# Weight buffers and activations in opposite 64-byte halves of SBUF

## The chip, the core and the metric

The kernel runs on one core of a Trainium2 chip. What is measured is the device time of one execution in microseconds (us). The kernel before takes 2329.44 us, the median of three runs (2329.22 to 2330.43).

## What is computed

The kernel computes a decoder trunk of two layers on 256 tokens of width 2048, in float32. Cut to the frame:

```python
h = x                                            # (1, 256, 2048)
for layer in range(2):
    u = rms_norm(h, norm_mix) @ w_in             # 2048 x 6160 (layer 0), 2048 x 7176 (layer 1)
    a, b = two_mixers(u)                         # layer 0: GLA and MoBA; layer 1: FoX and HGRN2
    h = h + concat([a, b]) @ w_out               # 2048 x 2048
    m = rms_norm(h, norm_mlp)
    h = h + square(relu(m @ w_up)) @ w_down      # 2048 x 8192, 8192 x 2048
return rms_norm(h, final_norm)
```

Two details matter for the change. MoBA adds an ALiBi bias, `-slope * (t - s)` under a causal mask, to its scores. FoX adds differences of a running sum of log forget gates over the 256 positions, `cumsum(log_f)`.

## The kernel before

**Three products for one.** Every large product is made of float32r matmuls. A weight tile `raw` is split into `wh` (rounded to float32r, ScalarE, L996) and `wl = raw - wh` (VectorE, L997), an activation in the same way into a high and a low part, and each product is high x wh + high x wl + low x wh, summed in PSUM.

**Units and blocks.** A unit is 128 rows of a weight matrix times 1024 columns (1040 or 1032 in the two blocks that carry a few extra columns, `extra`). A block is 16 units that sum into one set of accumulators; there are 49 blocks, 784 units. `fetch` (L981 to L998) loads the units in pairs into a `raw` buffer (three of them) and splits each into a `wh` and a `wl` buffer (six of each, handed out in turn). `fetch` runs two units ahead.

**Where the matmuls stand.** The loop at the end calls, for unit i, `step(0, i)` and then `step(1, i - 2)`: the first half of unit i's output (token rows or hidden columns), then the second half of unit i - 2. So between the first matmul of `step(0, i)` and that of `step(0, i + 1)` stand the matmuls of two units of one parity. There are two kinds:

- natural blocks (L1040): the activation is stationary (128 x 128) and the weights move, 512 columns at a time; 6 matmuls a step. In the blocks of `w_in` the activation is `xh` and `xl`; in those of `w_out` and `w_down` it is `mh0`, `ml0` for units 0 to 7 of a block and `mh1`, `ml1` for units 8 to 15.
- turned blocks (L1023, the sixteen of `w_up`): the weights are stationary and `xh` or `xl` moves, 256 columns at a time; 12 matmuls a step.

**Where the tiles lie.** The pools lay tiles one after another in each partition, every one at a multiple of 32 bytes. In the program as built these are the addresses, in bytes modulo 128:

| tiles | before | after |
|---|---|---|
| `wh` and `wl`, buffers 0, 2, 4 | 0 | 64 |
| `wh` and `wl`, buffers 1, 3, 5 | 64 | 64 |
| from one such buffer to the next | 4160 bytes | 4224 bytes |
| `raw` (three buffers) | 0 | 64 |
| `xh`, `xl`, `h`, `ident` | 0 | 0 |
| `mh0`, `ml0`, `ml1` | 0 | 0 |
| `mh1` | 64 | 0 |
| `stg` (two buffers) | 64 | 0 |
| `lev`, `at` | 0 | 64 |
| `v`, `sv`, `g` (tags S1, S2) | 0 | 64 |

Units 0, 2, 4, ... of a block use buffers 0, 2, 4 and units 1, 3, 5, ... buffers 1, 3, 5, since 16 is even. Inside a weight tile the matmuls start at multiples of 512 bytes, inside `xh`, `xl`, `mh`, `ml` too.

**Beside the matmuls** run the mixers' tasks, which the loop hands out in small pieces between units (`bg`). Three of them are touched: the constants made at the start (`const_task`), the ALiBi bias (`alibi`, L783, on GpSimd), and the running sum of the forget gates (`fox_forget`, three small matmuls with the triangular matrix `tri`, L803 to L805).

Of the kernel before, what the change touches and what calls it, by code (L numbers as in the profile page):

```python
# [8 lines left out]
F32 = mybir.dt.float32  # L9
F32R = mybir.dt.float32r  # L10
# [7 lines left out]
D = 2048  # L18
KT = D // P
CB = 1024  # L20
LAG = 2
AHEAD = 2
STARTN = 14
# [14 lines left out]
def trunk(ctx: ExitStack, tc: tile.TileContext, x, ev_norm_mix, ev_w_in, ev_gla_gate_w2, ev_gla_gate_b,  # L38
# [66 lines left out]
    def small(shape, name, bufs=2):  # L105
        return work.tile(shape, F32, name=name, tag=name, bufs=bufs)
# [11 lines left out]
    xl = cons.tile([P, KT, S], F32R, name="xl")  # L118
    h = cons.tile([P, 2, D], F32, name="h")
    mtiles.update({m: cons.tile([P, 256], U8, name=f"mask{m}") for m in LEVELS[4:]})  # L120
    tri = cons.tile([P, S], F32, name="tri")
    seg = cons.tile([P, S], F32, name="seg")

    dist = cons.tile([P, 384], F32, name="dist")


    xin = x[0].rearrange("(t p) d -> p t d", p=P)
# [41 lines left out]
    pool.memset(mhalf, -0.5)  # L169
    masks = {}  # L170

    def causal(tl):
        for c in (0, 256):
            pool.affine_select(out=tl[:, c:c + P], in_=tl[:, c:c + P], pattern=[[-1, P]], compare_op=ALU.is_ge,
                               fill=NEG, base=0, channel_multiplier=1)

    def const_task():

        pool.memset(tri, 1.0)
        pool.affine_select(out=tri[:, 0:P], in_=tri[:, 0:P], pattern=[[1, P]], compare_op=ALU.is_ge, fill=0.0, base=0,  # L180
                           channel_multiplier=-1)
        pool.memset(seg, 1.0)
        pool.memset(seg.rearrange("p (a b) -> p a b", b=64)[:, :, 0:1], 0.0)
        for m in LEVELS[1:]:
            yield from room(0, 1)
            nb = 64 // m
            mf = lev()[:, 0:64]
            mk = mtiles[m]
            mv = mf.rearrange("p (n m) -> p n m", m=m) if 1 < m < 64 else mf
            dims = [[2 * m, nb]] * (nb > 1) + [[0, m]] * (m > 1)  # L190
            pool.memset(mf, 1.0)
            pool.affine_select(out=mv, in_=mv, pattern=[[-a, b] for a, b in dims], compare_op=ALU.is_ge, fill=0.0,
                               base=0, channel_multiplier=1)
            pool.affine_select(out=mv, in_=mv, pattern=dims, compare_op=ALU.is_ge, fill=0.0, base=m - 1,
                               channel_multiplier=-1)
            yield BAR
            dve.tensor_copy(mk.rearrange("p (g c) -> p g c", c=64), mf.unsqueeze(1).to_broadcast([P, 4, 64]))
            lev_done()
            masks[m] = mk
            yield 0.3  # L200
        pool.iota(dist[:, 0:128], pattern=[[1, 128]], base=0, channel_multiplier=-1,
                  allow_small_or_imprecise_dtypes=True)
        pool.iota(dist[:, 128:384], pattern=[[1, 256]], base=-128, channel_multiplier=-1,
                  allow_small_or_imprecise_dtypes=True)
        causal(dist)
        yield BAR
        mx, e0, e1, sm = (small([P, 8], f"lb{i}", 1) for i in range(4))
        dve.tensor_tensor(mx, vec("lb0"), vec("lb1"), ALU.max)
        dve.tensor_sub(e0, vec("lb0"), mx)
        dve.tensor_sub(e1, vec("lb1"), mx)  # L210
        act.activation(e0, e0, AF.Exp)
        act.activation(e1, e1, AF.Exp)
        dve.tensor_add(sm, e0, e1)
        dve.reciprocal(sm, sm)
        dve.tensor_mul(e0, e0, sm)
        dve.tensor_mul(e1, e1, sm)
        dve.tensor_add(lb, e0, e1)
        dve.tensor_sub(lb, lb, e0)
        yield 1.0
# [26 lines left out]

    def norm_rstd(key):
        until(lambda: all((key, "ss", t, i) in written for t in range(2) for i in range(2)))
        r = small([P, 2], "rstd")
        pool.tensor_add(r, ssq[key][:, :, 0], ssq[key][:, :, 1])  # L250
        rsq(r, r, 2, 1.0 / D)
        return r
# [198 lines left out]
    def gla_out(at, v, g, dv, h0, nh, k0, gain, halves, key):  # L451

        yield from room(1)
        ps = aux()
        for i in range(nh):
            hd = h0 + i
            dg, off = at[hd // 2 * 2]
            c = slice(hd * dv, (hd + 1) * dv)
            o0 = ps[:, i * 2 * dv:i * 2 * dv + dv]
            o1 = ps[:, i * 2 * dv + dv:(i + 1) * 2 * dv]  # L460
            pe.matmul(o0, dg[:, 2 * (hd % 2)], v[:, 0, c], start=True, stop=True)
            pe.matmul(o1, off[:, hd % 2], v[:, 0, c], start=True, stop=False)
            pe.matmul(o1, dg[:, 2 * (hd % 2) + 1], v[:, 1, c], start=False, stop=True)
        yield BAR
        yield from room(0, 1)
        n = 2 * nh
        ss = small([P, 4], "oss")
        y = lev()
        for j in range(n):
            act.activation(y[:, j * dv:(j + 1) * dv], ps[:, j * dv:(j + 1) * dv], AF.Square, accum_out=ss[:, j:j + 1])  # L470
        yield BAR
        r = small([P, 4], "orr")
        rsq(r[:, 0:n], ss[:, 0:n], n, 1.0 / dv)
        yield BAR
        y = y.rearrange("p (t c) -> p t c", t=2)
        for j in range(n):
            i, t = divmod(j, 2)
            c = slice((h0 + i) * dv, (h0 + i + 1) * dv)
            dve.scalar_tensor_tensor(y[:, t, i * dv:(i + 1) * dv], ps[:, j * dv:(j + 1) * dv], r[:, j:j + 1],
                                     g[:, t, c], ALU.mult, ALU.mult)  # L480
        aux_done()
        yield 0.8
        yield BAR
        yield from room(1)
        pt = aux()
        for i in range(2):
            for t in range(2):
                pe.transpose(pt[:, i * 256 + t * P:i * 256 + (t + 1) * P], y[:, t, i * P:(i + 1) * P], ident)
        lev_done()
        yield BAR  # L490
        if 0 not in halves:
            halves[0] = mid(0)
        mh, ml = halves[0]
        for i in range(2):
            gg = gain[:, i:i + 1] if gain.shape[1] == 2 else gain[:, 0:1]
            act.activation(mh[:, k0 + i], pt[:, i * 256:(i + 1) * 256], AF.Identity, scale=gg)
        for i in range(2):
            gg = gain[:, i:i + 1] if gain.shape[1] == 2 else gain[:, 0:1]
            dve.scalar_tensor_tensor(ml[:, k0 + i], pt[:, i * 256:(i + 1) * 256], gg,
                                     mh[:, k0 + i].bitcast(F32), ALU.mult, ALU.subtract)  # L500
            written.add((key, k0 + i))
        aux_done()
        yield 0.8
# [78 lines left out]
    def mixers(lay):  # L582
# [33 lines left out]
        def gla_qk(acc, t):  # L616
            if t == 0:
                scales()
                st["q"] = scratch("mh0", 4, "gqT")
                kb = scratch("ml0", 8, "gkT")  # L620
                st["k"], st["b"] = kb[:, 0:4], kb[:, 4:8]
                st["d"] = small([P, 8, 2], "gdiag", 1)[:, 0:4]
            sg = stage()
            act.activation(sg[:, 0:512], acc[0], AF.Identity, scale=st["rq"][:, t:t + 1])
            dve.tensor_scalar(sg[:, 512:1024], acc[1], st["r"][:, t:t + 1], None, ALU.mult)
            tk["q", t] = spawn(heads_gen(sg, 0, 4, st["q"], t))
            tk["k", t] = spawn(heads_gen(sg, 4, 4, st["k"], t))

            def diag():
                yield from room(0, 1)  # L630
                junk = lev()
                for hd in range(4):
                    a, b = (sg[:, c + hd * P:c + (hd + 1) * P] for c in (0, 512))
                    dve.tensor_tensor_reduce(out=junk[:, hd * P:(hd + 1) * P], in0=a, in1=b, scale=1.0, scalar=0.0,
                                             op0=ALU.mult, op1=ALU.add, accum_out=st["d"][:, hd, t:t + 1])
                    yield 0.2
                lev_done()
            tk["d", t] = spawn(diag())
# [142 lines left out]
                                            tk["out"]))  # L781

        def alibi(hd, bt):  # L783
            pool.tensor_scalar(bt, dist, 2.0 ** -(hd + 1), None, ALU.mult)
            yield 0.05

        def fox_forget():
# [12 lines left out]
            yield BAR  # L800
            yield from room(1)
            pc = aux()
            pe.matmul(pc[:, 0:8], tri[:, 0:P], l[:, 0], start=True, stop=True)  # L803
            pe.matmul(pc[:, 8:16], tri[:, P:S], l[:, 0], start=True, stop=False)
            pe.matmul(pc[:, 8:16], tri[:, 0:P], l[:, 1], start=False, stop=True)  # L805
            yield BAR
            ct = small([P, 2, 8], "fct", 1)
            act.copy(ct, pc[:, 0:16].rearrange("p (t h) -> p t h", h=8))
# [172 lines left out]
    def fetch(i):  # L981
# [9 lines left out]
        raw = raws["cur"][:, j % 2]  # L991
        if i < 2:
            nc.sync.dma_start(raw, w[r0:r0 + P, cs])
        wh = wspl.tile([P, n], F32R, name="wh", tag="wh")
        wl = wspl.tile([P, n], F32R, name="wl", tag="wl")
        pin(act.activation(wh, raw, AF.Copy))  # L996
        pin(dve.tensor_sub(wl, raw, wh.bitcast(F32)))  # L997
        split[i] = (wh, wl)  # L998
# [117 lines left out]
```

## Time and profile before

| what | value |
|---|---|
| median of three runs | 2329.44 us |
| profiled execution, its own time | 2329.49 us |
| its span in the trace | 2327.8 us |
| TensorE busy | 2308.9 us, 99% |
| VectorE busy | 1285.5 us, 55% |
| ScalarE busy | 1086.3 us, 47% |
| GpSimd busy | 63.3 us, 3% |
| weights and activations moved | 418.68 MB, mean 180 GB/s |
| granted TensorE clock, mean | 0.998 |

A matmul's busy time in the trace overlaps that of the next, so the share says that TensorE always has work, not how fast it goes through it. In the timeline each row merges neighbouring instructions of one kind; its first number is the start of the first of them.

### The profile page before, as it was taken

The page shows a single profiled execution, that of the slowest core. Times are in us where ns is not written, and L with a number is a line of the kernel's source. Part 1 is how long each engine was busy: PE and PEld are TensorE (multiplying, and loading weights), DVE is VectorE, ACT ScalarE, POOL GpSimd, SP SyncE. Part 2 cuts the span into 40 slices and gives each one's busy share as a digit, 9 for nine tenths or more (in the row PEclk, how much of TensorE's full clock was granted, in tenths as well). Part 3 has the DMA queues.
Part 4 walks back from the last instruction along what each step waited for, and adds up shares of the span by engine and source line. Part 5 has one row for each costly group of instructions (what it writes and reads, how often), then busy time and mean ns, then how long its engine had stood idle before and what let it go on. Part 6 is the DMA issues. An engine that isn't in the chain of part 4 may idle for free.

```text
span 2327.8 us, 32679 instructions
## 1 busy us (share of the span) xinstructions
PE 2308.9 (99%) x13652; PEld 2026.2 (87%) x13652; DVE 1285.5 (55%) x1564; ACT 1086.3 (47%) x1370; POOL 63.3 (3%) x128
## 2 busy tenths in 40 slices
PE   8999999999999999999999999999999999999998
PEld 7888888998998998998887888788988988988986
DVE  5575545554554454465557775555554554555554
ACT  5464544443443353354446545644443443443443
POOL 2000100000000000000000000100000000000000
PEclk9999999999999999999999999999999999999999
DMA  7645545555555555555554434455555565555553
GB/s 242 193 150 162 163 159 185 181 183 198 182 192 188 189 191 186 194 183 184 183 180 160 162 127 163 150 183 187 186 186 195 183 194 185 192 188 191 189 184 124
DMA packets 110612, 418.68 MB, mean 180 GB/s; under 512 B 6814, under 2 KB 8944, under 8 KB 110336
## 3 DMA queue, kind: packets, MB, share of 16 engines
q1 hardware_dynamic: 109536, 415.46, 54.0%
q8 instruction: 107, 1.75, 0.3%
q10 hardware_dynamic: 608, 1.06, 0.1%
q14 instruction: 41, 0.34, 0.0%
q0 software_dynamic: 320, 0.07, 0.0%
HBM read 414.47 MB, written 2.10 MB: 179 GB/s over the span
## 4 chain that ended last, share of the span: by engine, by line
PE 98%; ACT 1%; DVE 1%; DMA 0%; SPq 0%; issue 0%; POOL 0%; POOLq 0%; ACTq 0%
PE acc L1040 61%; PE acc L1023 31%; PE aux L434 1%; PE aux L1040 1%; PE aux L273 1%; PE aux L335 0%; DMA raw<-in_ev_w_in_dram 0%; PE aux L512 0%; PE aux L536 0%; DVE hb L737 0%; ACT wh L996 0%; PE aux L511 0%; PE aux L427 0%; PE aux L558 0%; PE aux L557 0%; PE aux L367 0%
## 5 line engine op out<-in xcount | busy, mean ns | idle before, releaser
L997 DVE TENSOR_TENSOR wl<-raw,wh 128x1024 fp32r<-128x1024 f32 (+2 forms) x784 | 960.2, 1226 | 891.9 <-ACT wh L996 890.3
L996 ACT ACTIVATE wh<-raw 128x1024 fp32r<-128x1024 f32 (+2 forms) x784 | 830.3, 1060 | 1130.6 <-PE acc L1040 675.6
L1040 PE MATMUL acc<-wh,mh 128*128 128x512 f32 x1280 | 414.0, 394 | 0.0
L1040 PE MATMUL acc<-wh,ml 128*128 128x512 f32 x1280 | 412.4, 393 | 0.0
L1040 PE MATMUL acc<-wl,mh 128*128 128x512 f32 x1280 | 412.1, 393 | 0.0
L1023 PE MATMUL acc<-xh,wl 128*128 128x256 f32 x2048 | 353.9, 280 | 0.0
L1023 PE MATMUL acc<-xh,wh 128*128 128x256 f32 x2048 | 353.5, 279 | 0.0
L1023 PE MATMUL acc<-xl,wh 128*128 128x256 f32 x2048 | 353.1, 279 | 0.0
L1023 PEld LDWEIGHTS acc<-xh,wh 128*128 128x128 f32 x2048 | 290.6, 188 | 2.6
L1023 PEld LDWEIGHTS acc<-xh,wl 128*128 128x128 f32 x2048 | 289.5, 188 | 0.7
L1023 PEld LDWEIGHTS acc<-xl,wh 128*128 128x128 f32 x2048 | 289.0, 189 | 0.0
L1040 PEld LDWEIGHTS acc<-wh,ml 128*128 128x128 f32 x1280 | 240.2, 188 | 55.0
L1040 PEld LDWEIGHTS acc<-wl,mh 128*128 128x128 f32 x1280 | 240.4, 188 | 54.2
L1040 PEld LDWEIGHTS acc<-wh,mh 128*128 128x128 f32 x1280 | 238.0, 188 | 53.9 <-DVE stg L892 1.6
L1040 PE MATMUL acc<-wh,xh 128*128 128x512 f32 x832 | 272.3, 398 | 2.4 <-ACT xh L279 2.4
L1040 PE MATMUL acc<-wl,xh 128*128 128x512 f32 x832 | 262.9, 387 | 2.5 <-DVE wl L997 2.5
L1040 PE MATMUL acc<-wh,xl 128*128 128x512 f32 x832 | 261.7, 385 | 0.0
L1040 PEld LDWEIGHTS acc<-wl,xh 128*128 128x128 f32 x832 | 153.2, 189 | 34.2 <-DVE wl L997 3.8
L1040 PEld LDWEIGHTS acc<-wh,xl 128*128 128x128 f32 x832 | 153.2, 189 | 31.1
L1040 PEld LDWEIGHTS acc<-wh,xh 128*128 128x128 f32 x832 | 147.8, 189 | 28.6 <-ACT xh L279 3.3
L867 DVE TENSOR_TENSOR h<-acc,h 128x512 f32<-128x512 f32 x72 | 47.8, 685 | 20.5 <-PE acc L1040 20.5
L892 DVE SCALAR_TENSOR_TENSOR stg<-acc,rrow 128x512 f32<-128x512 f32 x64 | 42.4, 685 | 17.2 <-PE acc L1023 17.2
(239 smaller groups left out, 1006.1 us busy)
## 6 DMA issues: line engine op xcount, KB each, us to landing
raw<-in_ev_w_up_dram SPq DMA_DIRECT2D x64, 1024.0 KB, 4.9
raw<-in_ev_w_down_dram SPq DMA_DIRECT2D x64, 1024.0 KB, 5.5
raw<-in_od_w_up_dram SPq DMA_DIRECT2D x64, 1024.0 KB, 4.9
raw<-in_od_w_down_dram SPq DMA_DIRECT2D x64, 1024.0 KB, 5.5
raw<-in_od_w_in_dram SPq DMA_DIRECT2D x48, 1024.0 KB, 4.9
raw<-in_ev_w_in_dram SPq DMA_DIRECT2D x39, 1024.0 KB, 5.4
raw<-in_ev_w_out_dram SPq DMA_DIRECT2D x16, 1024.0 KB, 5.6
raw<-in_od_w_out_dram SPq DMA_DIRECT2D x16, 1024.0 KB, 5.5
```

What stands on the lines that cost most here:

```text
L273: pin(pe.transpose(ps[:, i * 256 + t * P:i * 256 + (t + 1) * P], h[:, t, kt * P:(kt + 1) * P], ident))
L434: pe.matmul(ps[:, i * 64:(i + 1) * 64], a, r, start=True, stop=True)
L867: dve.tensor_tensor(h[:, t, sl], acc[i], h[:, t, sl], ALU.add)
L892: dve.scalar_tensor_tensor(y, acc[i].rearrange("p (k s) -> p k s", s=S), 0.0, rr, ALU.max, ALU.mult)
L996: pin(act.activation(wh, raw, AF.Copy))
L997: pin(dve.tensor_sub(wl, raw, wh.bitcast(F32)))
L1023: pe.matmul(banks[o][:, k * S:(k + 1) * S], m[:, c0:c0 + P], a, start=j == 0 and p == 0 and k == 0, stop=j == n - 1 and p == 2 and k == 1, ...
L1040: pin(pe.matmul(o, a, m[:, c0:c1], start=first, stop=last))
```

## The change

All large weight buffers are made 4224 bytes long (`WB = 1056` columns of 4 bytes), of which 1024 to 1040 columns are used. The tiles ahead of them are cut so that the first buffer starts at 64 modulo 128; small tiles behind them grow so that the activations start at 0. `tri` keeps one 128 x 128 triangle instead of a triangle and a block of ones, and the ones are read with step 0 from a tile `one`. `dist` keeps 256 of its 384 columns; `alibi` multiplies these and copies the first 128 into the last 128.

```diff
+WB = 1056
...
-    tri = cons.tile([P, S], F32, name="tri")
+    tri = cons.tile([P, P], F32, name="tri")
+    one = cons.tile([P, 8], F32, name="one")
     seg = cons.tile([P, S], F32, name="seg")
 
-    dist = cons.tile([P, 384], F32, name="dist")
+    dist = cons.tile([P, 256], F32, name="dist")
+    cons.tile([P, 8], F32, name="pad2")
...
+        pool.memset(one, 1.0)
         pool.memset(tri, 1.0)
-        pool.affine_select(out=tri[:, 0:P], in_=tri[:, 0:P], pattern=[[1, P]], compare_op=ALU.is_ge, fill=0.0, base=0,
+        pool.affine_select(out=tri, in_=tri, pattern=[[1, P]], compare_op=ALU.is_ge, fill=0.0, base=0,
                            channel_multiplier=-1)
...
-        pool.iota(dist[:, 128:384], pattern=[[1, 256]], base=-128, channel_multiplier=-1,
+        pool.iota(dist[:, 128:256], pattern=[[1, 128]], base=-128, channel_multiplier=-1,
                   allow_small_or_imprecise_dtypes=True)
-        causal(dist)
+        causal(dist, (0,))
...
-        r = small([P, 2], "rstd")
+        r = small([P, 16], "rstd")[:, 0:2]
...
-        ss = small([P, 4], "oss")
+        ss = small([P, 16], "oss")
...
-                st["d"] = small([P, 8, 2], "gdiag", 1)[:, 0:4]
+                st["d"] = small([P, 16, 2], "gdiag", 1)[:, 0:4]
...
-            pool.tensor_scalar(bt, dist, 2.0 ** -(hd + 1), None, ALU.mult)
+            pool.tensor_scalar(bt[:, 0:256], dist, 2.0 ** -(hd + 1), None, ALU.mult)
+            pool.tensor_copy(bt[:, 256:384], bt[:, 0:128])
...
-            pe.matmul(pc[:, 0:8], tri[:, 0:P], l[:, 0], start=True, stop=True)
-            pe.matmul(pc[:, 8:16], tri[:, P:S], l[:, 0], start=True, stop=False)
-            pe.matmul(pc[:, 8:16], tri[:, 0:P], l[:, 1], start=False, stop=True)
+            pe.matmul(pc[:, 0:8], tri, l[:, 0], start=True, stop=True)
+            pe.matmul(pc[:, 8:16], one[:, 0:1].to_broadcast([P, P]), l[:, 0], start=True, stop=False)
+            pe.matmul(pc[:, 8:16], tri, l[:, 1], start=False, stop=True)
...
-        wh = wspl.tile([P, n], F32R, name="wh", tag="wh")
-        wl = wspl.tile([P, n], F32R, name="wl", tag="wl")
+        wh = wspl.tile([P, WB], F32R, name="wh", tag="wh")[:, 0:n]
+        wl = wspl.tile([P, WB], F32R, name="wl", tag="wl")[:, 0:n]
```

On VectorE, ScalarE and the DMA queue of SyncE the instructions stand in the same order before and after. On GpSimd the only rows that move are those of the constants and of the ALiBi biases. Before, the eight biases of layer 0 (`lev<-dist`) stand there in this way, between the output norms of the last GLA heads (`orr`) and the norm of the next stage (`rstd`):

```order
L245 TENSOR_TENSOR orr<-orr,mhalf 128x2
L784 TENSOR_SCALAR lev<-dist 128x384 x3
L244 TENSOR_SCALAR orr<-oss 128x2
L245 TENSOR_TENSOR orr<-orr,mhalf 128x2
L784 TENSOR_SCALAR lev<-dist 128x384 x5
L250 TENSOR_TENSOR rstd<-ssq 128x2
```

After, at the same place on GpSimd:

```order
L788 TENSOR_SCALAR lev<-dist 128x256 x2
L789 COPY lev<-lev 128x128 x2
L788 TENSOR_SCALAR lev<-dist 128x256
L248 TENSOR_SCALAR orr<-oss 128x2
L789 COPY lev<-lev 128x128
L249 TENSOR_TENSOR orr<-orr,mhalf 128x2
L788 TENSOR_SCALAR lev<-dist 128x256
L789 COPY lev<-lev 128x128
L788 TENSOR_SCALAR lev<-dist 128x256
L789 COPY lev<-lev 128x128
L788 TENSOR_SCALAR lev<-dist 128x256 x2
L789 COPY lev<-lev 128x128 x2
```

Each bias has become a shorter multiply and a copy; one multiply stands ahead of a norm that it followed with its copy behind. On TensorE one row differs in what it reads, the second of the three small matmuls of the forget gates in layer 1 (`fxl` is the log gate). After, it stands among its neighbours so:

```order
L1045 MATMUL acc_10009<-wh,xl 128x512
L1045 MATMUL acc_10010<-wh,xl 128x512
L808 MATMUL aux<-fxl,tri 128x8
L809 MATMUL aux<-fxl,one 128x8
L810 MATMUL aux<-fxl,tri 128x8
L339 MATMUL aux<-ident,stg 128x128 x4
```

Before, the same rows read `tri` three times, at the same place; nothing on TensorE has moved.

## Rows read from the trace of the kernel before

**Rows 1.** Page, part 1: busy us (share of the span) x instructions, by engine.

```profile
PE 2308.9 (99%) x13652; PEld 2026.2 (87%) x13652; DVE 1285.5 (55%) x1564; ACT 1086.3 (47%) x1370; POOL 63.3 (3%) x128
```

**Rows 2.** Largest waits of TensorE: for what, us in total, times, longest.

```profile
PE aux L1052 <- DMA vrow<-in_ev_norm_mix_dram: 3.7, 1, 3.7
PE acc L1040 <- DVE wl L997: 2.5, 2, 2.2
```

**Rows 3.** Timeline of VectorE around 1250 us: start us, us, instruction.

```profile
1246.42 4.54 DVE L737 TENSOR_TENSOR_SCAN hb<-seg,hb 128x256 f32<-128x256 f32 x5
1250.88 1.35 DVE L997 TENSOR_TENSOR wl<-raw,wh 128x1024 fp32r<-128x1024 f32 x1
```

**Rows 4.** Page, part 5: groups, count | busy, mean ns | idle before.

```profile
L1040 PE MATMUL acc<-wh,mh 128*128 128x512 f32 x1280 | 414.0, 394 | 0.0
...
L1023 PE MATMUL acc<-xh,wh 128*128 128x256 f32 x2048 | 353.5, 279 | 0.0
...
L1040 PE MATMUL acc<-wh,xh 128*128 128x512 f32 x832 | 272.3, 398 | 2.4 <-ACT xh L279 2.4
```

**Rows 5.** Timeline of TensorE, second up block of layer 0.

```profile
458.27 0.36 PE L1023 MATMUL acc<-xh,wh 128*128 128x256 f32 x1
...
477.95 0.62 PE L1023 MATMUL acc<-xh,wh 128*128 128x256 f32 x4
...
480.67 0.62 PE L1023 MATMUL acc<-xh,wh 128*128 128x256 f32 x4
...
483.51 0.64 PE L1023 MATMUL acc<-xh,wh 128*128 128x256 f32 x4
...
486.29 0.64 PE L1023 MATMUL acc<-xh,wh 128*128 128x256 f32 x4
...
489.13 0.63 PE L1023 MATMUL acc<-xh,wh 128*128 128x256 f32 x4
```

**Rows 6.** Timeline of TensorE, first down block of the third hidden quarter, layer 0.

```profile
870.89 0.62 PE L1040 MATMUL acc<-wh,mh 128*128 128x512 f32 x2
...
873.66 0.62 PE L1040 MATMUL acc<-wh,mh 128*128 128x512 f32 x2
...
876.41 0.64 PE L1040 MATMUL acc<-wh,mh 128*128 128x512 f32 x2
...
879.21 0.62 PE L1040 MATMUL acc<-wh,mh 128*128 128x512 f32 x2
...
881.97 0.63 PE L1040 MATMUL acc<-wh,mh 128*128 128x512 f32 x2
...
893.08 0.63 PE L1040 MATMUL acc<-wh,mh 128*128 128x512 f32 x2
...
895.84 0.62 PE L1040 MATMUL acc<-wh,mh 128*128 128x512 f32 x2
...
898.62 0.63 PE L1040 MATMUL acc<-wh,mh 128*128 128x512 f32 x2
...
901.39 0.39 PE L1040 MATMUL acc<-wh,mh 128*128 128x512 f32 x1
```

**Rows 7.** Groups by shape, the splits on VectorE; page, part 5, on ScalarE.

```profile
L997 DVE TENSOR_TENSOR wl<-raw,wh 128x1024 fp32r<-128x1024 f32 x752 | 920.7, 1225 | 853.2 <-ACT wh L996 851.6
...
L997 DVE TENSOR_TENSOR wl<-raw,wh 128x1040 fp32r<-128x1040 f32 x16 | 19.8, 1242 | 18.3 <-ACT wh L996 18.3
...
L996 ACT ACTIVATE wh<-raw 128x1024 fp32r<-128x1024 f32 (+2 forms) x784 | 830.3, 1060 | 1130.6 <-PE acc L1040 675.6
```

**Rows 8.** DMA issues: count, KB each, median us to landing.

```profile
raw<-in_ev_w_in_dram SPq DMA_DIRECT2D x39, 1024.0 KB, 5.4
...
raw<-in_ev_w_in_dram SPq DMA_DIRECT2D x8, 1040.0 KB, 5.4
```

**Rows 9.** Groups on GpSimd.

```profile
L784 POOL TENSOR_SCALAR lev<-dist 128x384 f32<-128x384 f32 x8 | 10.3, 1306 | 40.0 <-PE aux L536 33.5 <-PE aux L488 6.4
...
L394 POOL COPY lev<-hb 128x128 f32<-128x128 f32 x4 | 1.5, 386 | 18.3 <-PE aux L434 18.3
```

More of the change, by code (lines that the diff above doesn't have):

```diff
@@ L170, in trunk, with causal @@
     masks = {}
-    def causal(tl):
-        for c in (0, 256):
+    def causal(tl, cs=(0, 256)):
+        for c in cs:
             pool.affine_select(out=tl[:, c:c + P], in_=tl[:, c:c + P], pattern=[[-1, P]], compare_op=ALU.is_ge,
```

## The prediction

> **What bounds the kernel now.** I read the page's busy table first: TensorE is busy 99% of the span, VectorE 55%, ScalarE 47% [rows 1]. Then TensorE's waits, of which the two largest are 3.7 us for a first load at the start and 2.5 us for wl [rows 2]; 2.2 of these fall at 1250 us, where VectorE is first held by a row of scans [rows 3]. So the time is the number of matmuls times the distance from one start to the next, and the costliest groups give the numbers [rows 4]: 3 x 2048 = 6144 turned matmuls of 256 columns (weights stationary, xh or xl moving), 3 x 1280 = 3840 of 512 columns on mh or ml, 3 x 832 = 2496 of 512 columns on xh or xl (weights moving, activations stationary). The mean durations there overlap their neighbours; the pace has to be read from start times. So the view that matters is TensorE's timeline.
>
> The kernel before already holds both layouts side by side. A weight buffer is 4160 bytes, that is 65 x 64, so buffers 0, 2, 4 start at 0 mod 128 bytes and 1, 3, 5 at 64. Six buffers are handed out in turn and a block has 16 units, so even units of a block lie at 0 and odd units at 64. xh and xl lie at 0. mh0, ml0 and ml1 lie at 0, mh1 alone at 64.
>
> In an up block [rows 5] each row is the first of a unit's stretch of 24 matmuls; counted from the block's first matmul at 458.27 us, 477.95 begins unit 7. The differences are 2.72 (odd), 2.84 (even), 2.78 (odd), 2.84 us (even). Even: 5.68 us / 48 = 118.3 ns a matmul; odd: 5.50 / 48 = 114.6 ns. With weights in the other 64-byte half than xh and xl, a matmul is 3.75 ns faster.
>
> That could be a habit of odd units rather than of addresses. The down block [rows 6] tells these apart; a unit is 12 matmuls there and 870.89 begins unit 4. Units 4 to 7 read mh0 and ml0, both at 0: 2.77 and 2.80 us for even units (232.1 ns a matmul), 2.75 and 2.76 for odd ones (229.6 ns). Units 12 to 14 read mh1 at 64 and ml1 at 0: 2.76 and 2.77 for even units (230.4 ns), 2.78 for the odd one (231.7 ns). The order has turned round, and what turned is mh1's half. Four of six matmuls there are on mh1, so even units gain in most of them and odd ones lose. I take the relation between the two operands of TensorE as the cause: same half slow, other half fast.
>
> The Trainium skill's "SBUF — State Buffer", section "Who interferes with whom", states that TensorE has two read ports, for the moving operand and for the weight load, independent of each other, and that only the pair shared by VectorE and GpSimd causes contention. By that the halves could not matter and the change would give nothing; rows 5 and 6 disagree by 2.5 to 3.75 ns a matmul, and I go by the rows.
>
> **The change part by part.** After it all wh and wl buffers lie at 64 and xh, xl, mh0, ml0, mh1, ml1 at 0 mod 128, so every large matmul has the relation of the fast units.
>
> Turned matmuls: half of 6144 are in even units, 3072 x 3.75 ns = 11.5 us. Bounds from single pairs of rows 5: 2.84 against 2.78 is 2.5 ns (7.7 us), 2.84 against 2.72 is 5.0 ns (15.4 us).
>
> Matmuls on mh and ml: the four kinds of units are equally many and average (232.1 + 229.6 + 230.4 + 231.7) / 4 = 230.95 ns; all become the 229.6 of the odd early unit. 3840 x 1.35 ns = 5.2 us. Bounds: if the end value is 2.76 us a unit (230.0 ns), 3.6 us; if 2.75 (229.2 ns), 6.7 us.
>
> Matmuls on xh and xl with the weights moving: no long clean stretch of these is in my rows, since transposes and score matmuls of the mixers stand between. Their addresses are those of units 4 to 7 of rows 6, so half of 2496 go from 232.1 to 229.6: 1248 x 2.5 ns = 3.1 us; bounds by single pairs, 0.01 us and 0.05 us a unit, 1.0 to 5.2 us.
>
> VectorE and ScalarE read raw, which moves from 0 to 64. An odd unit's row of a 1040-column pair already began at 4160 bytes, 64 mod 128. Such pairs take 1242 ns a unit on VectorE against 1225 with 1024 columns, which is 17 ns for 16 columns more; ScalarE takes 1060 ns a unit over all [rows 7]. I cost the move at nothing: a unit is at least 2.72 us of TensorE, so on either engine even a tenth more stays hidden. The loads of these pairs landed in 5.4 us, the same as the plain ones of that matrix [rows 8]: nothing.
>
> GpSimd: each alibi bias was one multiply of 384 columns, 1.31 us, eight times; it becomes one of 256 and a copy of 128 columns, for which a copy of that size in layer 1 took 0.39 us [rows 9]. With the shorter multiply anywhere between nothing and 1.31 us, that is 0.9 us less to 0.4 us more a head, so at most 8 x 0.4 = 3 us on GpSimd; none of it is TensorE's, which has other matmuls then and has nothing of GpSimd's among its large waits [rows 2]. The ones and the smaller sum matrix and distance table cost nothing: GpSimd, 3% busy [rows 1], makes the constants early, and one 8-column matmul reads ones instead of a half of tri.
>
> Transposes: stg moves from 64 to 0 and lev from 0 to 64, against the identity at 0. In the program 112 lose and 80 gain; at the turned price of 3.75 ns that is 0.4 us against 0.3. Nothing.
>
> What may be late next is the wait of 2.2 us for wl, behind the scans of layer 1's gates on VectorE [rows 2, 3]. A block of 192 matmuls before it becomes about 0.2 us shorter, so the wait may grow by that. Elsewhere splits stay two units ahead.
>
> Sum: 11.5 + 5.2 + 3.1 = 19.8 us off the profiled execution's own 2329.5 us (span 2327.8 and 1.7 around it; the median of the runs is 2329.4): 2309.7, so I say 2310. All low ends together give 12.3 us (2317), all high ends 27.3 us (2302).
>
> **The rivals.** First, no change: the pace alternates with the unit for a reason that stays, say the row of the raw pair or the turn of the buffers, and the padding does nothing. For it: in up blocks parity and half can't be separated. Against it: the reversal in rows 6. It gives 2329. 5%. The independent ports of the Trainium skill's "SBUF — State Buffer" (the section above) would give the same.
>
> Second, slower: what has to lie apart is the weights and raw. Raw was at 0 throughout, so weights at 64 (odd units) were apart from it; after the change raw is at 64 too, and every unit would have the even units' pace. Turned: 3072 x 3.75 = 11.5 us more; mh and ml: from 230.95 to 232.1, 4.4 us more; the rest 3.1 more: 2348. It decides if ScalarE's and VectorE's reads of raw, which run beside nearly every matmul, disturb TensorE. For it: again parity in the up blocks. Against: in units 12 and 14 raw and the weights are both at 0, and those units are the fast ones. 4%.
>
> Third, less than the sum: the pace of a fast unit is partly owed to its slow neighbours (TensorE's queue of loaded weights evens out distances), or the gain holds for turned matmuls alone. That gives 2329.5 - 11.5 = 2318 or a little above, up to 2325. 6%.
>
> **How the numbers follow.** The forecast, with the bounds above, gets 85%, of which I leave 3% for below 2302. The range is 2302 to 2318: the ends of the sum, with 1 us above for the wait of layer 1. What a measurement here can tell from no change is 0.2%, 4.7 us. Faster by more: forecast and third rival, 0.91. Within: 0.05. Slower: 0.04.
>
> **What would show it.** In the profile after: stretches of 24 turned matmuls at about 2.75 us in every unit, with no alternation, and of 12 matmuls in down blocks at about 2.755 us throughout both halves of a block; an up block of 384 about 0.7 us shorter, a down block of 192 about 0.26 us. TensorE's waits stay those of before, and splits keep 1.06 and 1.23 us. It is wrong if units still alternate (first rival), if all take 2.84 us (second), or if the stretches are shorter but a new wait stands in TensorE's list.

## The result and the profile after

The kernel after takes 2313.97 us (median of 6 runs, 2313.8 to 2314.34), the kernel before 2329.33 us beside it (6 runs, 2328.4 to 2330.43): a ratio of 0.9935 [0.9924, 0.9945], 15.4 us less. The forecast was 2310 with a range of 2302 to 2318. The time falls into the range, but the profile shows that the 15.4 us are not the sum that was forecast: one term is larger, two are missing. All runs of this document that were profiled had a granted clock of 0.998 or 0.999 of the full one.

Page of the kernel after, part 1, answering to [rows 1]; its span is 2312.3 us, 15.5 less:

```profile
PE 2293.0 (99%) x13652; PEld 2009.5 (87%) x13652; DVE 1285.3 (56%) x1564; ACT 1086.5 (47%) x1370; POOL 62.2 (3%) x136
```

TensorE's largest waits in it (what for, us in total, times, longest), answering to [rows 2]:

```profile
PE aux L1057 <- DMA vrow<-in_ev_norm_mix_dram: 3.7, 1, 3.7
PE acc L1045 <- ACT xh L283: 3.1, 2, 2.4
PE acc L1045 <- DVE wl L1002: 2.6, 3, 2.2
```

TensorE is still busy 99%, and no wait has come in: 3.7 us for the first load, 2.6 (before 2.5) for `wl` with the longest at 2.2 as before, 3.1 for `xh` at the starts of stages (before 2.4). So the whole gain is in the distance from one matmul's start to the next.

Timeline of TensorE in the second up block of layer 0 (start us, busy us, instruction), answering to [rows 5]. The first row is the block's first matmul, the next five are the first of the stretches of units 7 to 11, the last is the first matmul of the next block:

```profile
457.80 0.34 PE L1028 MATMUL acc<-xh,wh 128*128 128x256 f32 x1
...
477.22 0.62 PE L1028 MATMUL acc<-xh,wh 128*128 128x256 f32 x4
...
479.94 0.62 PE L1028 MATMUL acc<-xh,wh 128*128 128x256 f32 x4
...
482.66 0.62 PE L1028 MATMUL acc<-xh,wh 128*128 128x256 f32 x4
...
485.38 0.62 PE L1028 MATMUL acc<-xh,wh 128*128 128x256 f32 x4
...
488.10 0.62 PE L1028 MATMUL acc<-xh,wh 128*128 128x256 f32 x4
...
501.71 0.39 PE L1045 MATMUL acc<-wh,mh 128*128 128x512 f32 x1
```

Every stretch of 24 takes 2.72 us: 113.3 ns a matmul, with no alternation between even and odd units. Before, even units took 118.3 and odd units 114.6. The block takes 501.71 - 457.80 = 43.91 us; before, from 458.27 to 503.05, 44.78. That the once fast odd units are faster too was not forecast.

In the first up block of a hidden quarter (here the second quarter of layer 0) it begins otherwise; the rows are the first of units 3 to 6:

```profile
598.87 0.63 PE L1028 MATMUL acc<-xh,wh 128*128 128x256 f32 x4
...
601.70 0.63 PE L1028 MATMUL acc<-xh,wh 128*128 128x256 f32 x4
...
604.52 0.62 PE L1028 MATMUL acc<-xh,wh 128*128 128x256 f32 x4
...
607.24 0.62 PE L1028 MATMUL acc<-xh,wh 128*128 128x256 f32 x4
```

Units 3 and 4 take 2.83 and 2.82 us (117.7 ns), one of either parity, and from unit 5 on a stretch takes 2.72. Six of the eight hidden quarters begin in this way. In the first quarter of each layer it is the second up block that runs at 118.0 and 117.7 ns in units 1 and 2 and at 113.3 to 113.4 from unit 3 on. So an up block can change its pace on the way, while its addresses take the same turns.

Timeline of TensorE in the first down block of the third hidden quarter, answering to [rows 6]; units 4 to 8, then 12 to 14:

```profile
865.60 0.62 PE L1045 MATMUL acc<-wh,mh 128*128 128x512 f32 x2
...
868.35 0.62 PE L1045 MATMUL acc<-wh,mh 128*128 128x512 f32 x2
...
871.14 0.62 PE L1045 MATMUL acc<-wh,mh 128*128 128x512 f32 x2
...
873.89 0.62 PE L1045 MATMUL acc<-wh,mh 128*128 128x512 f32 x2
...
876.68 0.62 PE L1045 MATMUL acc<-wh,mh 128*128 128x512 f32 x2
...
887.76 0.62 PE L1045 MATMUL acc<-wh,mh 128*128 128x512 f32 x2
...
890.51 0.62 PE L1045 MATMUL acc<-wh,mh 128*128 128x512 f32 x2
...
893.30 0.62 PE L1045 MATMUL acc<-wh,mh 128*128 128x512 f32 x2
```

Here the alternation has stayed: 2.75 (even), 2.79 (odd), 2.75, 2.79 us, and 2.75, 2.79 in the second half of the block: 229.2 and 232.5 ns. Before, the second half of a block had the opposite sign; now both halves have one. The mean of the two is 230.8 ns, that of before was 230.95.

From the first matmul of each block in the timeline to that of the next, summed by kind of block (us):

| blocks | matmuls move | before | after | forecast of the difference | measured |
|---|---|---|---|---|---|
| 16 of `w_up` | `xh`, `xl` (turned) | 721.3 | 705.9 | -11.5 | -15.4 |
| 16 of `w_down`, 4 of `w_out` | weights, past `mh`, `ml` | 714.7 + 192.9 | 714.6 + 193.0 | -5.2 | 0.0 |
| 13 of `w_in` | weights, past `xh`, `xl` | 680.9 | 681.3 | -3.1 | +0.4 |

Splits on the page of after, part 5 (count, busy us, mean ns, idle before), answering to [rows 7], and the ALiBi biases in the groups on GpSimd, answering to [rows 9]:

```profile
L1002 DVE TENSOR_TENSOR wl<-raw,wh 128x1024 fp32r<-128x1024 f32 (+2 forms) x784 | 960.1, 1226 | 879.4 <-ACT wh L1001 877.3
L1001 ACT ACTIVATE wh<-raw 128x1024 fp32r<-128x1024 f32 (+2 forms) x784 | 830.6, 1061 | 1115.8 <-PE acc L1045 675.2
```

```profile
L788 POOL TENSOR_SCALAR lev<-dist 128x256 f32<-128x256 f32 x8 | 6.8, 856 | 39.9 <-PE aux L540 33.1 <-PE aux L492 6.6
...
L789 POOL COPY lev<-lev 128x128 f32<-128x128 f32 x8 | 3.9, 505 | 0.2
```

VectorE's split takes 1226 ns over all shapes, ScalarE's 1061 (1060 before): moving `raw` by 64 bytes cost nothing. A bias takes 856 + 505 = 1361 ns instead of 1306, 0.06 us more a head, and nothing waits for it.

### The profile page after: what moved, and what is told of

Read it like the earlier page. It is cut to its first block, busy times and chain, and to the rows that moved or that the text cites. A ratio compares the mean times of both kernels' runs of the same rounds, so it can differ in the third digit from the quotient of the medians.

```text
span 2312.3 us, 32691 instructions
## 1 busy us (share of the span) xinstructions
PE 2293.0 (99%) x13652; PEld 2009.5 (87%) x13652; DVE 1285.3 (56%) x1564; ACT 1086.5 (47%) x1370; POOL 62.2 (3%) x136
## 3 DMA queue, kind: packets, MB, share of 16 engines
q10 hardware_dynamic: 608, 1.06, 0.1%
## 4 chain that ended last, share of the span: by engine, by line
PE 97%; ACT 1%; DVE 1%; DMA 0%; SPq 0%; issue 0%; POOL 0%; POOLq 0%; ACTq 0%
PE acc L1045 61%; PE acc L1028 30%; PE aux L438 1%; PE aux L1045 1%; PE aux L277 1%; PE aux L339 1%; DMA raw<-in_ev_w_in_dram 0%; PE aux L516 0%; ACT wh L1001 0%; PE aux L540 0%; DVE wl L1002 0%; PE aux L515 0%; PE aux L431 0%; PE aux L561 0%; PE aux L371 0%; PE aux L560 0%
## 5 line engine op out<-in xcount | busy, mean ns | idle before, releaser
L1002 DVE TENSOR_TENSOR wl<-raw,wh 128x1024 fp32r<-128x1024 f32 (+2 forms) x784 | 960.1, 1226 | 879.4 <-ACT wh L1001 877.3
L1001 ACT ACTIVATE wh<-raw 128x1024 fp32r<-128x1024 f32 (+2 forms) x784 | 830.6, 1061 | 1115.8 <-PE acc L1045 675.2
L1028 PE MATMUL acc<-xh,wh 128*128 128x256 f32 x2048 | 348.8, 277 | 0.0
L1028 PE MATMUL acc<-xl,wh 128*128 128x256 f32 x2048 | 347.9, 277 | 0.0
L1028 PE MATMUL acc<-xh,wl 128*128 128x256 f32 x2048 | 347.9, 277 | 0.0
```

The lines of the kernel that those rows point to most:

```text
L1028: pe.matmul(banks[o][:, k * S:(k + 1) * S], m[:, c0:c0 + P], a, start=j == 0 and p == 0 and k == 0, stop=j == n - 1 and p == 2 and k == 1, ...
```

## The experiments

The table of addresses ahead of the prediction is modulo 128. Modulo 256 it reads otherwise. Before, the buffers of one kind are 4160 bytes apart, 64 mod 256, and run through all four of 0, 64, 128, 192; `wh` and `wl` of one unit are 128 apart. After, they are 4224 apart, 128 mod 256: `wh` and `wl` of even units lie at 192, those of odd units at 64, `xh` and `xl` at 0, `mh0`, `ml0`, `mh1`, `ml1` at 128. Below, "distance" is the address of what moves minus the address of what is stationary, mod 256. After, it is 64 in even and 192 in odd units of down blocks, and 192 in even and 64 in odd units of the `w_in` blocks.

The theory ("theory A" in the expectations): the distance mod 256 sets the pace, and 64 is fast for the natural matmuls, 192 slow. Its first rival ("theory B"): the 64-byte half alone counts, and what still alternates is the parity of the unit, by the turn of the buffers or the rows of the `raw` pair.

**Move mh and ml by 128.** Neither half nor parity changes, the distance in the down blocks does.

```diff
+    work.tile([P, 32], F32, name="pad3", tag="pad3")
...
-        mn = small([P, 2], "smx", 6)
+        mn = small([P, 2], "smx", 5)
```

> The activations mh0, ml0, mh1, ml1 (and stg, lev before them) move up by 128 bytes, so their 64-byte half stays the same; xh, xl and the weights stay. Theory A (a natural matmul's pace follows the address of its moving weights minus that of its stationary activation, modulo 256: 64 fast, 192 slow): in down blocks the alternation turns round, even units go from 229.3 to 233 ns a matmul and odd units from 232.6 to 229.3; blocks on xh and xl and up blocks stay as after the change; time unchanged, 2314 us. Theory B (only the 64-byte half counts, and what still alternates is the unit's parity, by its buffers or its row of the raw pair): even units stay at 229.3, odd ones at 232.6.

One run: 2313.87 us. The same down block, units 4 to 7:

```profile
865.37 0.62 PE L1046 MATMUL acc<-wh,mh 128*128 128x512 f32 x2
...
868.16 0.62 PE L1046 MATMUL acc<-wh,mh 128*128 128x512 f32 x2
...
870.91 0.62 PE L1046 MATMUL acc<-wh,mh 128*128 128x512 f32 x2
...
873.70 0.62 PE L1046 MATMUL acc<-wh,mh 128*128 128x512 f32 x2
```

Even units now take 2.79, odd ones 2.75 and so on: the alternation has turned round, while the blocks of `w_in`, whose operands did not move, kept theirs (medians 232.4 even, 229.2 odd, of the stretches with hardly any other matmul in them). Parity is out, and the half cannot do it; the distance mod 256 fits. The sum stays (714.6 us for the down blocks), since half of the units have each distance in either case.

**All weights at one place mod 256.** Buffers 4096 bytes apart, all at 64 (or all at 192), the 16 or 8 extra columns in small tiles of their own (all at 192 needs two paddings more):

```diff
-            n = (512 + extra) // 2
-            self.cuts = ((0, 512), (512, 512 + n), (512 + n, 1024 + extra)) if extra else ((0, 512), (512, 1024))
+            self.cuts = ((0, 512), (512, 1024)) + (((1024, 1024 + extra),) if extra else ())
...
+        wh = wspl.tile([P, CB], F32R, name="wh", tag="wh")
+        wl = wspl.tile([P, CB], F32R, name="wl", tag="wl")
...
+            whx = wspl.tile([P, 16], F32R, name="whx", tag="whx")[:, 0:b.extra]
+            wlx = wspl.tile([P, 16], F32R, name="wlx", tag="wlx")[:, 0:b.extra]
```

> All weight buffers 4096 bytes apart (the 16 or 8 extra columns of two blocks in small tiles of their own), so that moving minus stationary is 64 modulo 256 in every natural matmul. Theory A: every natural matmul takes about 229.2 ns where half of them took 233 after the change; 6336 x 1.95 ns = 12.4 us less than after the change, 2301.6 us; down blocks 44.0 us instead of 44.4, no alternation; up blocks as after the change. Theory B: the same halves, so 2314 us, and units still alternate.

> As the kernel with all distances at 64, but weights 128 bytes further, so that moving minus stationary is 192 modulo 256 in every natural matmul. Theory A: every natural matmul takes about 233 ns, 12 us more than after the change, 2326 us; up blocks as after the change (64 and 192 were alike there). Theory B: the same halves, 2314 us.

At 64: 2326.82 us (11 runs, 2324.85 to 2333.52), ratio 0.9992 [0.9983, 1.0001]. At 192: 2368.28 us (4 runs, 2364.41 to 2369.71), ratio 1.0165 [1.0151, 1.0179]. Both times are off the expectations (2301.6 and 2326 us), but the natural matmuls do what the theory says: 229.0 ns in every unit at 64 (down blocks 708.7 us), 233.3 at 192 (721.6). Units 4 to 6 of the same down block, with the weights at 64 and then at 192:

```profile
873.34 0.62 PE L1052 MATMUL acc<-wh,mh 128*128 128x512 f32 x2
...
876.09 0.62 PE L1052 MATMUL acc<-wh,mh 128*128 128x512 f32 x2
...
878.84 0.62 PE L1052 MATMUL acc<-wh,mh 128*128 128x512 f32 x2
```

```profile
886.17 0.63 PE L1053 MATMUL acc<-wh,mh 128*128 128x512 f32 x2
...
888.97 0.63 PE L1053 MATMUL acc<-wh,mh 128*128 128x512 f32 x2
...
891.77 0.63 PE L1053 MATMUL acc<-wh,mh 128*128 128x512 f32 x2
```

2.75 us for each unit against 2.80, and no alternation in either. Two things were missed. The first is the price of the arrangement itself, in groups of the kernel at 64, with one of the groups that they replace in the kernel after below:

```profile
L1052 PE MATMUL aux<-whx,xh 128*128 128x16 f32 x32 | 5.6, 174 | 0.0
L1052 PE MATMUL aux<-whx,xh 128*128 128x8 f32 x32 | 5.4, 168 | 0.0
```

```profile
L1045 PE MATMUL aux<-wh,xh 128*128 128x264 f32 x32 | 9.1, 284 | 0.0
```

The number of matmuls is the same; in the two blocks with extra columns, 192 rows of three are cut into 512 + 512 + 16 (or 8) columns where they were 512 + 264 + 264 (or 260). The two blocks went from 47.4 to 56.3 and from 47.1 to 56.1 us: some 93 ns for a row of as many columns, 17.9 us in all, which hid the gain. The narrow matmul itself is short, 27 ns to the next start; the wide one behind it takes 315 ns instead of 229 (medians of start times). The second is the up blocks. At 192 fourteen of sixteen ran at 117.8 ns throughout and two at 113.5; at 64 three of sixteen ran at 117.6, thirteen at 113.4. With all turned matmuls of a kernel alike, there are still two paces, each kept for a whole block.

**The weights alone.** Without the small paddings behind the weights (`rstd`, `oss`, `gdiag`):

```diff
-        r = small([P, 16], "rstd")[:, 0:2]
+        r = small([P, 2], "rstd")
...
-        ss = small([P, 16], "oss")
+        ss = small([P, 4], "oss")
...
-                st["d"] = small([P, 16, 2], "gdiag", 1)[:, 0:4]
+                st["d"] = small([P, 8, 2], "gdiag", 1)[:, 0:4]
```

> The weights' part of the change alone: the small tiles are not padded, so mh0 and ml0 lie at 64 modulo 256, mh1 at 0 and ml1 at 192; weights at 192 (even units) and 64 (odd). Up blocks gain as in the change under either theory. Theory A, down blocks: units 0 to 7 even 232.4 ns (distance 128), odd 230.9 (distance 0); units 8 to 15 even 232.4 (192 on mh1, 0 on ml1), odd 230.3 (64 on mh1, 128 on ml1); mean 231.5, so 1.3 us more than after the change: 2315 us. Theory B: units 0 to 7 share the half and take 232 in even and odd units alike, units 8 to 15 are between, 230.5; mean 231.3.

2316.31 us (4 runs, 2315.13 to 2316.39), ratio 0.9943 [0.9928, 0.9958]. `mh0` and `ml0` lie at 64, `mh1` at 0, `ml1` at 192. The same down block, units 4 and 5:

```profile
865.83 0.62 PE L1045 MATMUL acc<-wh,mh 128*128 128x512 f32 x2
...
868.62 0.63 PE L1045 MATMUL acc<-wh,mh 128*128 128x512 f32 x2
...
871.36 0.62 PE L1045 MATMUL acc<-wh,mh 128*128 128x512 f32 x2
```

Even units (weights at 192, distance 128) take 2.79, odd ones (at 64, distance 0) 2.74 us, where 230.9 ns or 2.77 us was expected: "the same half" is the fastest so far, where the prediction calls it slow. In the second half of the block, where `mh1` and `ml1` differ, odd units ran at 231.9 ns where 230.3 was expected: the mean of two distances does not give the pace of their mixture. So of the 15.4 us the wide weight buffers with the rest of the change are worth some 13, and the small paddings about 2.

**All at 64, without the narrow matmuls (all64_whole, the 4352-byte kernel).** Buffers of 4352 bytes, 17 x 256, whole units as before; the room comes from masks kept once instead of four times, a bfloat16 `seg` and one small buffer less:

```diff
-WB = 1056
+WB = 1088
...
-    mtiles = {m: cons.tile([P, 256], U8, name=f"mask{m}") for m in LEVELS[1:4]}
+    mtiles = {m: cons.tile([P, 64], U8, name=f"mask{m}") for m in LEVELS[1:4]}
...
-    seg = cons.tile([P, S], F32, name="seg")
+    seg = cons.tile([P, S], mybir.dt.bfloat16, name="seg")
```

> Distance 64 in all natural matmuls as before (down blocks 229.0 ns), but with buffers of 4352 bytes that hold the extra columns too, so the 17.8 us which the small matmuls cost in the two blocks with extra columns go: 2326.8 - 17.8 = 2309 us. Theory L (turned matmuls run in one of two locked paces, 113.3 or 117.8 ns; with one distance throughout, a block keeps the pace that it starts with): some of the sixteen up blocks run at 117.8 as a whole, the others at 113.4, and the time differs from run to run by 1.7 us for each such block, 2304 to 2312. Rival M (each distance has its own mean pace): all up blocks alike at 114.2.

2306.80 us (4 runs, 2303.66 to 2309.15), ratio 0.9903 [0.989, 0.9917]: faster than both kernels. Natural blocks go to 228.9 ns in every unit (down 708.6, `w_in` 677.9 us). Neighbouring buffers lie 256 apart modulo 512 here and in one place modulo 4096 in the kernel at 64 with narrow matmuls, at the same pace, so nothing beyond the address modulo 256 shows. Units 7 and 8 of the first up block of layer 0 in its profile, and after them units 7 and 8 of the second, the same code on the same addresses:

```profile
431.54 0.63 PE L1028 MATMUL acc<-xh,wh 128*128 128x256 f32 x4
...
434.36 0.64 PE L1028 MATMUL acc<-xh,wh 128*128 128x256 f32 x4
```

```profile
476.52 0.62 PE L1028 MATMUL acc<-xh,wh 128*128 128x256 f32 x4
...
479.25 0.62 PE L1028 MATMUL acc<-xh,wh 128*128 128x256 f32 x4
```

2.82 us against 2.73 for a unit. The first block ran at 117.8 ns a matmul from unit 3 to unit 12, the second at 113.3. In this profile (2303.66 us) two of sixteen up blocks are slow; each costs about 384 x 4.5 ns = 1.7 us, so the spread of its runs, 5.5 us, would be that of three such blocks. Only one of these runs left a trace, so this is not shown. The kernel after has no such spread (0.5 us).

**Does a mixed distance decide the pace of an up block?** `xl` moved by 128, so that the turned distance changes between the matmuls of one unit (192 for `xh`, 64 for `xl`), with the weights at 64 and at 192 (`h`, which lies behind `xl`, moves along). Against the 4352-byte kernel:

```diff
+    cons.tile([P, 32], F32, name="pad4")
...
-    cons.tile([P, 56], F32, name="pad2")
+    cons.tile([P, 24], F32, name="pad2")
```

> As the kernel with distance 64 and whole buffers, and xl moves up by 128 bytes, so that in up blocks the distance alternates within each unit (192 on xh, 64 on xl, moving minus stationary). Theory L: the change of distance lets no block stay at 117.8; all sixteen up blocks at about 113.5 as after the change or better, the runs agree within 0.5 us. The matmuls on xl in the blocks of w_in pay for it, 832 x 4 ns = 3.3 us. 2304 + 3 = 2307 us. Rival M: xl's matmuls go to the pace of the kernel with all distances at 192 (117.2), so up blocks take (8 x 114.2 + 4 x 117.2) / 12 = 115.2 ns: 6 us more, 2318 us.

> As the kernel with all distances at 192, whose up blocks mostly ran at 117.8 ns, and xl moves up by 128 bytes, so that the distance of turned matmuls alternates within a unit (64 on xh, 192 on xl). Theory L: up blocks fall to about 113.5 to 114 ns, 724.8 to about 706 us for the sixteen; time 2368.3 - 19 = 2349 us, less about 3 us that xl's natural matmuls gain (distance 64). Rival M: (8 x 117.2 + 4 x 114.2) / 12 = 116.2 ns, 718 us for the sixteen.

2330.40 us (11 runs, 2329.41 to 2331.3), ratio 1.0005 [0.9996, 1.0014], and 2367.67 us (one run). In both, all sixteen up blocks are slow (727.8 and 727.7 us). The first kernel was expected at 2307 us by one theory and 2318 by the other, the up blocks of the second at 706 and 718, and all of these missed. Unit 7 of the second up block of layer 0 with the weights at 64:

```profile
478.63 0.63 PE L1029 MATMUL acc<-xh,wh 128*128 128x256 f32 x4
...
481.46 0.63 PE L1029 MATMUL acc<-xh,wh 128*128 128x256 f32 x4
```

2.83 us. Where the distance changes from unit to unit (the change itself), most of a block is fast; where it changes inside a unit, none is. The theory that any alternation of 64 and 192 frees a block from the slow pace is out.

**Other distances.** Buffers 4096 apart with the narrow matmuls as above, all weights at 32, 0 (all0), 96 and 128, the activations at 0; only two paddings differ:

```diff
-    cons.tile([P, 72], F32, name="pad2")
+    cons.tile([P, 24], F32, name="pad2")
...
-    work.tile([P, 32], F32, name="pad3", tag="pad3")
+    work.tile([P, 16], F32, name="pad3", tag="pad3")
```

(this is the edit from 192 to 0).

> As the kernel with all distances at 64 (small tiles for the extra columns), with the weights 32 bytes lower: moving minus stationary is 32 modulo 256 in natural matmuls. If the pace follows the distance in steps of 64 bytes, as if such blocks were the places that two reads compete for, natural matmuls take 231 ns (the 0 of the kernel before) or 229 (64); if it follows smoothly, about 230. Turned matmuls: 113.3 or 117.8 block by block under theory L.

> As the kernel with all distances at 64 (small tiles for the extra columns), weights at 0: the same 64-byte half as every activation. The forecast's own premise (same half slow, other half fast): turned matmuls at 118.5 ns, natural ones at 232, as the even units of the kernel before. Were the half of no account and only the alternation of the kernel before slow, turned matmuls would take 113 to 115 and natural ones 229 to 230.

> As the kernel with all distances at 64 (small tiles for the extra columns), weights at 96 modulo 256. If natural matmuls are fast in a band around 64, as 229 ns; if 64 alone is fast (32 was as slow as 192), 233 ns. Turned matmuls: mostly 113.3 in whole blocks if the fast pace can hold there, 118 in all blocks if not, as at 32.

> As the kernel with all distances at 64 (small tiles for the extra columns), weights at 128 modulo 256: again the same 64-byte half. Same half slow: turned matmuls about 118 ns, natural ones 232.4, as where the kernel before had this distance.

One run each: 2370.89 (32), 2350.04 (0), 2372.51 (96), 2375.05 us (128). Weights at 0, unit 7 of the second up block and unit 4 of the down block of [rows 6]:

```profile
485.50 0.64 PE L1035 MATMUL acc<-xh,wh 128*128 128x256 f32 x4
...
488.38 0.64 PE L1035 MATMUL acc<-xh,wh 128*128 128x256 f32 x4
```

```profile
881.39 0.62 PE L1053 MATMUL acc<-wh,mh 128*128 128x512 f32 x2
...
884.11 0.62 PE L1053 MATMUL acc<-wh,mh 128*128 128x512 f32 x2
```

The turned matmuls are at their slowest (2.88 us a unit, 120.0 ns in all sixteen blocks), and the natural ones at their fastest, 2.72 us or 227.0 ns. Same place, opposite effects. The expectations were met in part. At 32 none of the natural paces named came (229, 230 or 231). At 0 the turned half of the premise held and the natural half was reversed. At 96 both slow paces came, at 128 nearly so.

The table has them together with 64 and 192 of the same arrangement, as means over a block. `raw` moves along with the weights in all six, so the distance between these two, which the second rival of the prediction is about, is the same in all while the paces differ:

| distance of natural matmuls mod 256 | ns, down blocks | turned: weights at | ns, up blocks |
|---|---|---|---|
| 0 | 227.0 | 0 | 120.0 in all |
| 32 | 233.3 | 32 | 118.3 in all |
| 64 | 229.0 | 64 | 113.4 in thirteen, 117.6 in three |
| 96 | 233.3 | 96 | 118.6 in fourteen, 117.4 in two |
| 128 | 233.0 | 128 | 120.0 in ten, 118.7 in six |
| 192 | 233.3 | 192 | 117.8 in fourteen, 113.5 in two |

**The best of both.** From this table: weights at 64 for the turned ones, `mh` and `ml` moved to 64 so that their distance is 0. Against the 4352-byte kernel, whose `pad2` shrinks by 192 bytes while three small tiles change their pool:

```diff
+    few8, fxe, fxl = (cons.tile([P, 2, 8], F32, name=n) for n in ("few8", "fxe", "fxl"))
...
+    work.tile([P, 16], F32, name="pad3", tag="pad3")
```

> As all64_whole (weights at 64 mod 256, 4352 bytes apart, xh and xl at 0), but mh0, ml0, mh1 and ml1 moved by 64 bytes, so that moving minus stationary is 0 mod 256 for the 3840 matmuls of 512 columns on mh and ml and stays 64 for the 2496 on xh and xl; the turned ones keep 192. If the distance of the two operands sets the pace of each kind by itself: the 3840 go from 228.9 ns to the 227.0 that all0 had, 7.3 us less than all64_whole: 2306.8 - 7.3 = 2299.5 us (2296 to 2302, by how many up blocks keep the slower of their two paces), down blocks of 43.9 us instead of 44.3. Rival: the 227.0 of all0 came from all operands, xh and xl too, lying at one place, or from the absolute address; then mh and ml stay at 228.9 or become as slow as 232: 2307 to 2319 us.

2315.65 us (5 runs, 2312.8 to 2317.49), ratio 0.9939 [0.9926, 0.9953]: 8.9 us slower than the kernel it was made from, where 7.3 less was expected. Unit 4 of the down block, and unit 7 of the first up block of the second quarter:

```profile
864.93 0.61 PE L1047 MATMUL acc<-wh,mh 128*128 128x512 f32 x2
...
867.65 0.61 PE L1047 MATMUL acc<-wh,mh 128*128 128x512 f32 x2
```

```profile
605.58 0.63 PE L1030 MATMUL acc<-xh,wh 128*128 128x256 f32 x4
...
608.40 0.64 PE L1030 MATMUL acc<-xh,wh 128*128 128x256 f32 x4
```

The down blocks do what was expected: 2.72 us a unit, 226.8 ns; down and `w_out` blocks together 892.9 us against 900.2, 7.3 less. So for natural matmuls the distance is what counts, not the address (both operands lie at 64 here, both at 0 in the kernel with all weights at 0). But the up blocks, whose operands lie as in the 4352-byte kernel, now run at 117.5 to 117.8 in thirteen of sixteen (723.2 us against 705.8, 17.4 more).

Start times show where the two kernels part. In the first up block after a down block, steps of the two alternate at first. In quarters two to four the 4352-byte kernel falls from 118 to 113 ns within each of these steps and then stays at 113; here the up block stays at 118 once the last step of the down block is done. The second up block of a quarter goes on at the pace of the first in both kernels. It has one gap, of 182 to 186 ns at its seventh matmul, in the 4352-byte kernel, where it is fast before and behind it; here the gap is missing. The first two up blocks of each layer are mixed: three of the four are fast here, two in the 4352-byte kernel, with gaps of 180 to 202 ns near their start in both. So what stands before an up block seems to have part in which pace it gets. No run tested this, and two rivals stand: the edit moved `stg`, `lev`, `at` and `v` by 64 bytes too, and the two kernels ran on different chips (the kernel before took 2329.5 and 2329.6 us beside them).

## Why the prediction was right, and where it was wrong

**What bounds the kernel: right.** TensorE's pace was the whole of it: in three kernels that differ in two paddings alone (weights at 0, 64 and 192), the down blocks ran at 227.0, 229.0 and 233.3 ns. The Trainium skill's "SBUF — State Buffer", section "Who interferes with whom", has the two reads of TensorE independent. These runs do not bear that out as far as the pace goes. What part of the chip does this, no run here shows.

**"Same half slow, other half fast": wrong for the natural matmuls.** Distances 64 and 192 are both "other half", and are 229.0 and 233.3; distance 0, the same place, is the fastest at 227.0. In the kernel before, `wh` and `wl` of a unit lay 128 apart, so that every unit mixed two distances: 64 with 192 in odd early units (229.6), 0 with 128 in even ones (232.1). I read the pace of such a mixture as that of a half. The evidence was sound as far as it went (that an address can turn the alternation round, as in [rows 6], the run that moved `mh` and `ml` by 128 shows), but I worked out the addresses modulo 128, because the buffers alternate by 64. Modulo 256 the program before has four places, and units that I called alike were not. By the prediction's own sign, "wrong if units still alternate", the natural half of it failed. For the turned matmuls the rule holds in its direction: 113.3 to 117.8 ns at 64 and 192, 118.7 to 120.0 at 0 and 128.

**Turned term: mis-sized.** 11.5 forecast, 15.4 measured, the upper bound by chance. Only even units were to gain. In fact 113.3 ns is a pace of its own below the 114.6 of the odd units: 3072 x 5.0 ns + 3072 x 1.3 ns = 19.4 us if every matmul ran at it. By the start times, some 900 of the 6144 are still at about 117.7 in the kernel after, most of them at the start of the six first up blocks described above and of the first two of each layer; that takes back 900 x 4.4 ns = 4.0 us. The third rival ties fast units to slow neighbours; what was measured has the opposite sign, fast units that got faster with their neighbours. Why is not shown.

**Terms of mh/ml and of xh/xl with moving weights: 5.2 and 3.1 forecast, 0.0 and -0.4 measured.** The step that failed is "all become the 229.6 of the odd early unit": half became 229.2, half 232.5, as much gained as lost. (The count of 2496 holds 192 of 264 or 260 columns, which changes its term by less than 0.3 us.) The 4352-byte kernel, which gives every unit distance 64, shows what the terms would have been: 714.7 - 708.6 + 192.9 - 191.6 = 7.4 us and 680.9 - 677.9 = 3.0 us. So in result the third rival's second half came true (the gain holds for turned matmuls alone), at 2314 instead of "2318 or a little above", and the forecast's time came within 4 us by luck: two errors of opposite sign, 3.9 us too little and 8.7 too much.

**Costs at nothing: right.** Splits 1.06 and 1.23 us, no new wait; GpSimd 0.06 us a head within the bounds of -0.9 to 0.4 (the copy took 0.51 us where 0.39 was taken); loads of `w_in` land in 5.5 us (5.4). The wait behind the scans of layer 1 stayed at 2.2 us.

**Still open:** what it is in the addresses of the two operands that sets the pace, and what puts an up block into one of its two paces. Whether the natural mixtures add up from their parts was not settled: the second half of the down blocks in the weights-alone kernel does not fit.

## What to carry to other kernels

Where TensorE is the bound and never waits, compare the start times of equal matmuls unit by unit; an alternation of 1 to 4% was worth more here than any wait in the list. Tabulate both operands' addresses modulo 256 at least, and modulo the spacing of the buffers, before a rule is made of what alternates. A layout that makes every unit alike (buffer spacing a multiple of 256 bytes) is the one in which a pace can be read, and here the one that won, 2306.8 us, but only with the right place: a spacing of 4096 bytes took 2326.8 us with the weights at 64 and 2350 to 2375 us with them at 0, 32, 96, 128 or 192, in each case with about 18 us for the narrow matmuls.

## What the runs showed of the hardware that was not expected

- Float32r matmuls of 512 columns ran at 226.8 to 233.3 ns by nothing but the distance of their operands, at a granted clock of 0.998 to 0.999. Those of 256 columns ran at 113.3 to 120.0 ns, by the distance and by something more that stays open. The best distance of the one kind, 0, is the worst of the other.
- A stream of equal turned matmuls at distance 64 or 192 has two paces, 113.3 and 117.8 ns. With one distance throughout, a block mostly keeps one of them; in the kernel after, some blocks went from the slow to the fast one on the way. The kernels with all weights at 64 and `xh`, `xl` at 0 had 4.7 to 8.7 us between their fastest and slowest run, where the kernel before had 2.0 and the one with `xl` moved, slow in every up block, 1.9.
- A row of matmuls of 512 + 512 + 16 columns took some 93 ns longer than one of 512 + 264 + 264: the wide matmul behind the narrow one took 315 ns instead of 229.
